# A one-core trunk layer: 512-column gate products over four token tiles, the last layer norm tiles on VectorE, state-space products later in the queue

## The chip, the cores and the metric

The kernel runs as one program on one core of a Trainium2 chip. The metric is device time in microseconds. A profiled execution gives one trace with a span from its first to its last instruction; the timed runs are taken without a profile. Engines: TensorE (PE in rows, PEld for its weight loads), VectorE (DVE), ScalarE (ACT), GpSimd (POOL), SyncE (SP, which issues the DMAs).

## The reference, cut to what matters

One layer on x (1024 tokens x 1024), all float32. `z = x @ w_in` gives the streams of three branches: u and v (512 wide) with a gate g for the gated MLP, x_b with its gate for the state-space branch, q with its gate for attention over 256 memory tokens.

```python
def spatial_gating(u, v, w_s, b_s, ln_g, ln_b, causal):
    vh = layer_norm(v.reshape(Bsz, L, GM_HEADS, GM_HEAD_DIM), ln_g, ln_b)
    ...
    mixed = jnp.einsum('hts,bcshd->bcthd', w, vc) + b_s.T[None, None, :, :, None]
    return u * mixed.reshape(Bsz, L, GM_WIDTH)
...
        z = x @ w_in[layer]
        u_a, v_a, g_a, x_b, g_b, q_x, g_x = jnp.split(z, SPLITS, axis=-1)
        y_a = spatial_gating(jax.nn.gelu(u_a), jax.nn.gelu(v_a), ...)
        y_b = s5_branch(x_b, ...)
        y_x = memory_cross_attention(q_x, mem, xa_w_k[layer], xa_w_v[layer])
        y = jnp.concatenate([y_a * jax.nn.silu(g_a), y_b * jax.nn.silu(g_b),
                             y_x * jax.nn.silu(g_x)], axis=-1)
        x = layer_norm(DN_ALPHA * x + y @ w_out[layer], ln_g[layer], ln_b[layer])
```

The layer norm inside the spatial gate is per head (4 heads of 128 channels) and the mixing is per chunk of 128 tokens and head; in the state-space branch there are 16 groups of 64 complex states.

## The kernel before

Every large product is made of three matmuls with operands in the fp32r type (`mm3`, lines 144 to 146): a value is split into a high part (a cast on ScalarE, line 65) and a low part (a subtraction on VectorE, line 62), and high x high, high x low and low x high are summed in a PSUM bank. Weights come in **pieces** of 128 x 512: a load on SP, then the cast and the subtraction. There are four raw buffers and six pairs of high and low buffers, used in turn.

The input projection runs as **units** one after the other (`run_units`). A unit made by `fm` computes 128 channels for all 1024 tokens: weights stationary, 512 tokens moving, two z banks (there are four, used in turn; four more u banks serve everything else). A unit made by `tm` computes 256 gate channels v: a 128-token tile of x stationary, 256 weight columns moving; two token tiles share one bank, and the bank is finished (16 x 3 matmuls) before the next is begun. Its four pieces, two k tiles each, are needed for every token tile. The order of units is xb0, xb1, gb0, gb1, v0, u0, u1, g0, g1, v1, u2, u3, g2, g3, where gb is the state-space branch's gate, u and g those of the gated MLP.

Between the matmuls of units other work is put in by generators: at each `tick` a virtual clock `now` moves on, and generators whose time has come emit their next step. They are the attention (during xb and gb), the state-space batches (`ssm_batch`, four of them; pp and kp, then up, then yp are their matmuls; H is the state that yp reads, and comes from up through some ten VectorE steps), the normalisation and mixing of v (`mix_all`, matmuls mx), and the state-space gate (`glu_all`, matmuls gl; its operands yth and ytl come from yT, a copy of the transposes yt). `yield 4.0` says how far `now` must move until a step. The emission fixes TensorE's order; in this stage the order on the other engines and on SP is made by the scheduler of the framework. During the output projection the order is the written one on VectorE, ScalarE and GpSimd too.

`v_evac` takes a finished v bank: Gelu on ScalarE into `nv`, then statistics on VectorE, four instructions of each of two kinds. `mix_all` normalises in sixteen 128 x 128 steps on VectorE, after a power on GpSimd, and mixes.

The output projection goes over the columns 0 to 511 in eight banks at once, k by k (o0), then over columns 512 to 1023 tile by tile (o10 to o16), and for the last token tile in two quarters of 256 (o170, o171). `o_part` adds the residual and takes statistics, `finish_a(t)` aggregates, has GpSimd take the power, and multiplies; `finish_b(t)` scales, adds the bias and stores. For tiles 0 to 5 it scales on ScalarE and adds on GpSimd; tile 6 is done on VectorE in two halves; of tile 7, columns 864 to 1023 go by way of ScalarE and GpSimd and the rest is done on VectorE.

Of the kernel before, what the change touches and what calls it, by code (L numbers as in the profile page):

```python
# [36 lines left out]
def trunk_kernel(ctx, tc, xT, x, w_gq, w_kv, memT, w_fm, w_v, w_o,  # L37
# [127 lines left out]
    class Unit:  # L165
        def __init__(self, name, src, count, run):
            self.name, self.src, self.count, self.run = name, src, count, run
            self.pcs = []
# [6 lines left out]
    def run_units(units, after):  # L175
        for i, u in enumerate(units):
            u.fetch()
            u.run(u, units[i + 1] if i + 1 < len(units) else after)
# [470 lines left out]
    for hp in range(2):  # L649
        for lt in range(8):  # L650
# [5 lines left out]
    v_units = [tm(w_v[:, vb], f"v{vb}",  # L656
                  lambda t, kt: (xh[:, kt, tok[t]], xl[:, kt, tok[t]]),
                  lambda tt, ps, vb=vb: v_evac(vb, tt, ps), lambda vb=vb: v_done(vb))
               for vb in range(2)]
# [19 lines left out]
    def ssm_batch(bi):  # L679
# [80 lines left out]
        yield 4.0  # L760
# [70 lines left out]
    def v_evac(vb, tt, ps):  # L831
        if tt == 0:
            nv[vb] = gm.tile([P, 8, 256], F32, tag="nv", name=f"nv{vb}")
            stt[vb] = (gm.tile([P, 16, 6], F32, tag="stt", name=f"stt{vb}"),
                       gm.tile([P, 16, 2], F32, tag="mv", name=f"mv{vb}"),
                       gm.tile([P, 16], F32, tag="rsv", name=f"rsv{vb}"))
        t = nv[vb]
        st, mv, _ = stt[vb]
        S.activation(t[:, 2 * tt:2 * tt + 2].rearrange("p c f -> p (c f)"), ps,
                     AF.Gelu_apprx_tanh)  # L840
        for i in range(4 * tt, 4 * tt + 4):
            V.bn_stats(st[:, i], t[:, i // 2, tok[i % 2]])
        for i in range(4 * tt, 4 * tt + 4):
            V.bn_aggr(mv[:, i], st[:, i])

    def v_done(vb):
        spawn(mix_all(vb))

    def mix_all(vb):
        t = nv[vb]  # L850
        _, mv, rs = stt[vb]
# [3 lines left out]
        for h in range(2):  # L855
            for c in range(8):
                i = c * 2 + h
                sl = t[:, c, tok[h]]
                V.tensor_scalar(sl, sl, mv[:, i, 0:1], rs[:, i:i + 1], op0=ALU.subtract,
                                op1=ALU.mult)  # L860
            yield 2.0
        yield 4.0
        for h in range(2):
            hd = vb * 2 + h
            while hd not in have_u:
                yield 1.0
            for cq in range(2):
                ps = ubank(f"mx{hd}{cq}")
                for c in range(4):
                    T.matmul(ps[:, tok[c]], lhsT=t[:, cq * 4 + c, tok[h]], rhs=wT[:, hd],  # L870
                             start=(c == 0), stop=(c == 3), skip_group_check=True)
                now[0] += 0.85
                mt = gm.tile([P, 4, P], F32, tag="mt", bufs=2, name=f"mt{hd}{cq}")
                V.scalar_tensor_tensor(mt, ps.rearrange("p (c t) -> p c t", c=4),
                                       gmg[:, hd:hd + 1],
                                       tbias[:, hd].unsqueeze(1).to_broadcast([P, 4, P]),
                                       op0=ALU.mult, op1=ALU.add)
                mul(V, ya[:, hd, half[cq]], ya[:, hd, half[cq]], mt.rearrange("p c t -> p (c t)"))
                yield 2.0
# [19 lines left out]
    run_units([v_units[0], us[0], us[1], gs_[0], gs_[1], v_units[1], us[2], us[3]], gs_[2])  # L899
# [36 lines left out]
    def finish_a(t, n):  # L936
        mv, rs = stat[:, 192 + 4 * t:194 + 4 * t], stat[:, 194 + 4 * t:195 + 4 * t]
        V.bn_aggr(mv, ost[:, t, 0:n].rearrange("p a b -> p (a b)"))
        V.tensor_scalar(rs, mv[:, 1:2], LN_EPS, None, op0=ALU.add)  # L939
        G.tensor_tensor(rs, rs, nhalf[:, 0:1], op=ALU.pow)  # L940
        w = 864 if t == 7 else 1024
        V.scalar_tensor_tensor(res[:, t, :w], res[:, t, :w], mv[:, 0:1], lng[:, :w],
                               op0=ALU.subtract, op1=ALU.mult)

    def finish_b(t):
        rs = stat[:, 194 + 4 * t:195 + 4 * t]
        ot = res[:, t]
        if t < 6:
            S.activation(ot, ot, AF.Copy, scale=rs)  # L949
            add(G, ot, ot, lnb2)  # L950
            nc.sync.dma_start(out=out[tok[t]], in_=ot)
            return
        cuts = ((0, 512), (512, 1024)) if t == 6 else ((864, 1024), (0, 432), (432, 864))
        for a, b in cuts:
            if b - a > 160:
                V.scalar_tensor_tensor(ot[:, a:b], ot[:, a:b], rs, lnb2[:, a:b],
                                       op0=ALU.mult, op1=ALU.add)
            else:
                nm = stat[:, 195 + 4 * t:196 + 4 * t]
                V.scalar_tensor_tensor(nm, stat[:, 192 + 4 * t:193 + 4 * t], -1.0, rs,  # L960
                                       op0=ALU.mult, op1=ALU.mult)
# [71 lines left out]
def _layout(np, x, mem, w_in, gm_w_s, gm_b_s, gm_ln_g, gm_ln_b, ssm_lam_re, ssm_lam_im,  # L1033
# [14 lines left out]
    def both(a):  # L1048
# [13 lines left out]
        w_v=np.stack([cols(w[:, 512:768]), cols(w[:, 768:1024])], axis=1),  # L1062
# [39 lines left out]
```

## Time and profile before

| | us |
|---|---|
| median of 3 runs | 391.1 |
| lowest and highest run | 391.07, 392.14 |
| profiled execution | 391.75 |
| its span | 389.9 |

| engine | busy us | share of the span |
|---|---|---|
| TensorE, matmuls | 379.0 | 97% |
| TensorE, weight loads | 329.8 | 85% |
| VectorE | 267.5 | 69% |
| ScalarE | 155.0 | 40% |
| GpSimd | 101.1 | 26% |

Times of rows count from the start of the span. Matmuls are pipelined, so a row's own duration is longer than its share of the queue: what one costs is the distance between the starts of neighbours. Weight loads run beside matmuls. An engine runs its instructions in order; the wait of one holds up those behind it.

### The profile page before, as it was taken

The page shows a single profiled execution, that of the slowest core. Times are in us where ns is not written, and L with a number is a line of the kernel's source. Part 1 is how long each engine was busy: PE and PEld are TensorE (multiplying, and loading weights), DVE is VectorE, ACT ScalarE, POOL GpSimd, SP SyncE. Part 2 cuts the span into 40 slices and gives each one's busy share as a digit, 9 for nine tenths or more (in the row PEclk, how much of TensorE's full clock was granted, in tenths as well). Part 3 has the DMA queues.
Part 4 walks back from the last instruction along what each step waited for, and adds up shares of the span by engine and source line. Part 5 has one row for each costly group of instructions (what it writes and reads, how often), then busy time and mean ns, then how long its engine had stood idle before and what let it go on. Part 6 is the DMA issues. An engine that isn't in the chain of part 4 may idle for free.

```text
span 389.9 us, 5809 instructions
## 1 busy us (share of the span) xinstructions
PE 379.0 (97%) x2129; PEld 329.8 (85%) x2129; DVE 267.5 (69%) x580; ACT 155.0 (40%) x301; POOL 101.1 (26%) x80
## 2 busy tenths in 40 slices
PE   8999999999999999999999999999999999999990
PEld 6888898888888999888889999888888888888890
DVE  4599897888884689699769258855357410974475
ACT  4573596667673723131153224216346410012210
POOL 1315000000000865803936402300000000026763
PEclk9999999999999999999999999999999999999996
DMA  7883336312930100312111003200138710002124
GB/s 235 274 280 128 114 109 191 109 71 78 114 62 28 29 13 3 109 31 70 51 43 55 2 15 109 108 2 2 53 109 319 283 46 0 0 2 83 79 110 161
DMA packets 22189, 35.89 MB, mean 92 GB/s; under 512 B 5376, under 2 KB 8848, under 8 KB 22032
## 3 DMA queue, kind: packets, MB, share of 16 engines
q1 hardware_dynamic: 22160, 35.51, 29.9%
q8 instruction: 17, 0.28, 0.3%
q14 instruction: 12, 0.10, 0.1%
HBM read 29.67 MB, written 5.24 MB: 90 GB/s over the span
## 4 chain that ended last, share of the span: by engine, by line
PE 94%; POOL 2%; issue 1%; DMA 1%; DVE 1%; SPq 0%; POOLq 0%; ACT 0%
PE o L146 7%; PE o L145 7%; PE o L144 7%; PE zv L145 4%; PE zv L144 4%; PE zv L146 4%; PE zu L152 4%; PE zu L151 4%; PE zg L152 4%; PE zg L151 4%; PE zu L154 4%; PE zg L154 4%; PE av L615 2%; PE zgb L152 2%; PE zgb L154 2%; PE zxb L152 2%
## 5 line engine op out<-in xcount | busy, mean ns | idle before, releaser
L940 POOL TENSOR_TENSOR stat<-stat,nhalf 128x1 f32<-128x1 f32 x8 | 11.9, 1490 | 105.2 <-DVE stat L939 105.2
L145 PE MATMUL o<-l_wo,yh 128*128 128x512 f32 (+1 forms) x100 | 38.4, 384 | 0.0
L144 PE MATMUL o<-h_wo,yh 128*128 128x512 f32 (+1 forms) x100 | 38.4, 384 | 0.0
L146 PE MATMUL o<-h_wo,yl 128*128 128x512 f32 (+1 forms) x100 | 38.3, 383 | 0.0
L144 PE MATMUL zv<-h_v,xh 128*128 128x256 f32 x128 | 36.7, 286 | 0.0
L145 PE MATMUL zv<-l_v,xh 128*128 128x256 f32 x128 | 36.3, 283 | 0.0
L146 PE MATMUL zv<-h_v,xl 128*128 128x256 f32 x128 | 36.3, 283 | 0.0
L151 PE MATMUL zu<-xh,h_u 128*128 128x512 f32 x64 | 25.8, 403 | 0.0
L151 PE MATMUL zg<-xh,h_g 128*128 128x512 f32 x64 | 25.5, 399 | 0.0
L152 PE MATMUL zu<-xl,h_u 128*128 128x512 f32 x64 | 25.1, 391 | 0.0
L152 PE MATMUL zg<-xl,h_g 128*128 128x512 f32 x64 | 25.0, 391 | 0.0
L145 PEld LDWEIGHTS zv<-l_v,xh 128*128 128x128 f32 x128 | 24.6, 192 | 0.1
L144 PEld LDWEIGHTS zv<-h_v,xh 128*128 128x128 f32 x128 | 24.6, 192 | 0.1
L146 PEld LDWEIGHTS zv<-h_v,xl 128*128 128x128 f32 x128 | 24.5, 192 | 0.0
L968 DVE SCALAR_TENSOR_TENSOR res<-res,o 128x512 f32<-128x512 f32 (+1 forms) x16 | 10.3, 646 | 19.0 <-PE o L146 19.0
L949 ACT ACTIVATE res<-res,stat 128x1024 f32<-128x1024 f32 x6 | 6.9, 1152 | 41.0 <-POOL stat L940 41.0
L146 PEld LDWEIGHTS o<-h_wo,yl 128*128 128x128 f32 x100 | 18.8, 188 | 3.9
L145 PEld LDWEIGHTS o<-l_wo,yh 128*128 128x128 f32 x100 | 18.8, 188 | 3.9
L144 PEld LDWEIGHTS o<-h_wo,yh 128*128 128x128 f32 x100 | 18.8, 188 | 3.9
L154 PE MATMUL zu<-xh,l_u 128*128 128x512 f32 x64 | 19.8, 390 | 0.0
L154 PE MATMUL zg<-xh,l_g 128*128 128x512 f32 x64 | 19.8, 390 | 0.0
L676 POOL MEMSET M<- 128x512 f32 x2 | 1.0, 526 | 66.7 <-PE zgb L152 66.7
(301 smaller groups left out, 1073.2 us busy)
## 6 DMA issues: line engine op xcount, KB each, us to landing
r_wo<-in_w_o_dram SPq DMA_DIRECT2D x16, 256.0 KB, 3.0
res<-in_x_dram SPq DMA_DIRECT2D x8, 512.0 KB, 7.1
r_x<-in_xT_dram SPq DMA_DIRECT2D x15, 256.0 KB, 4.6
out_dram<-res SPq DMA_DIRECT2D x6, 512.0 KB, 2.6
r_v<-in_w_v_dram SPq DMA_DIRECT2D x8, 256.0 KB, 3.1
r_u<-in_w_fm_dram SPq DMA_DIRECT2D x8, 256.0 KB, 2.8
r_g<-in_w_fm_dram SPq DMA_DIRECT2D x8, 256.0 KB, 2.7
r_wgq<-in_w_gq_dram SPq DMA_DIRECT2D x7, 256.0 KB, 5.3
```

What stands on the lines that cost most here:

```text
L144: T.matmul(ps, lhsT=sh, rhs=mh, start=start, stop=False, **kw)
L145: T.matmul(ps, lhsT=sh, rhs=ml, start=False, stop=False, **kw)
L146: T.matmul(ps, lhsT=sl, rhs=mh, start=False, stop=stop, **kw)
L151: T.matmul(ps[h], lhsT=wh, rhs=xh[:, kt, half[h]], start=first, stop=False, **kw[h])
L152: T.matmul(ps[h], lhsT=wh, rhs=xl[:, kt, half[h]], start=False, stop=False, **kw[h])
L154: T.matmul(ps[h], lhsT=wl, rhs=xh[:, kt, half[h]], start=False, stop=last, **kw[h])
L615: T.matmul(ps[:, h * 256:h * 256 + 256], lhsT=vs[:, m, 2 * hp + h], rhs=pp[:, h * 2 + m], start=h + m + n == 0, stop=h + m + n == 3, skip_ ...
L676: G.memset(t, 0.0)
L940: G.tensor_tensor(rs, rs, nhalf[:, 0:1], op=ALU.pow)
L949: S.activation(ot, ot, AF.Copy, scale=rs)
L968: V.scalar_tensor_tensor(res[:, t, c0:c0 + w], res[:, t, c0:c0 + w], ALPHA, ps[:, :w], op0=ALU.mult, op1=ALU.add)
```

## The change

The gate units are cut the other way: a unit `vu(h)` computes all 512 channels of v for four token tiles (512 tokens), with 512 weight columns moving and four banks open; six k tiles run over all four tiles, the last two are run tile by tile, so that the banks finish one after the other. A piece is now one k tile with 512 columns; there are eight in a unit, fetched a few steps ahead of their use, and the weights are read once by each unit. The units are ordered v0, u0, u1, u2, u3, v1, g0, g1, g2, g3. Normalising and mixing follow the new cut. The wait ahead of yp is 6.0 in place of 4.0. In the tail tiles 0 to 4 are done as before, tile 5 on VectorE in one step, tile 6 on VectorE in two halves, tile 7 on VectorE in three pieces of 480, 352 and 192 columns.

```diff
     class Unit:
-        def __init__(self, name, src, count, run):
+        def __init__(self, name, src, count, run, ahead=8):
...
-            u.fetch()
+            u.fetch(u.ahead)
             u.run(u, units[i + 1] if i + 1 < len(units) else after)
...
-    def tm(src, name, stat, evac, done=None):
+    def vu(h, evac, done):
+
+
         def run(u, nxt):
-            for tt in range(4):
-                ps = zbank(f"z{name}{tt}")
-                for t2 in range(2):
-                    for kt in range(KT):
-                        wh, wl = u.pcs[kt // 2]
-                        cs = slice((kt % 2) * 256, (kt % 2) * 256 + 256)
-                        sh, sl = stat(2 * tt + t2, kt)
-                        mm3(ps[:, t2 * 256:t2 * 256 + 256], sh, sl, wh[:, cs], wl[:, cs],
-                            kt == 0 and t2 == 0, kt == KT - 1 and t2 == 1, chk=True)
...
-                            tick(1.3)
-                if tt in (1, 2) and nxt is not None:
-                    nxt.fetch(tt)
-        return Unit(name, lambda i: src[:, i], 4, run)
+            ps = [zbank(f"zv{h}{t}") for t in range(4)]
+
+            def mm(t, kt):
+                ts = slice((4 * h + t) * P, (4 * h + t) * P + P)
+                mm3(ps[t], xh[:, kt, ts], xl[:, kt, ts], *u.pcs[kt], kt == 0, kt == KT - 1)
+
+            for kt in range(KT - 2):
+                u.fetch(kt + 4)
+                for t in range(4):
+                    mm(t, kt)
+                    if t % 2:
+                        tick(1.36)
+            for t in range(4):
+                for kt in (KT - 2, KT - 1):
+                    mm(t, kt)
+                evac(t, ps[t])
+                if t == 3:
+                    done()
+                tick(1.36)
+                if t in (1, 2) and nxt is not None:
+                    nxt.fetch(t)
+        return Unit(f"v{h}", lambda i: w_v[:, i], KT, run, 4)
...
         add(V, H[:, :, 1:P], H[:, :, 1:P], jg[:, :, 0:P - 1])
-        yield 4.0
+        yield 6.0
         yps = ubank(f"yp{bi}")
...
+    def v_evac(th, t, ps):
...
+        S.activation(v[:, t], ps, AF.Gelu_apprx_tanh)
+        for i in range(4 * t, 4 * t + 4):
+            V.bn_stats(st[:, i], v[:, t, tok[i % 4]])
+        for i in range(4 * t, 4 * t + 4):
             V.bn_aggr(mv[:, i], st[:, i])
...
-    run_units([v_units[0], us[0], us[1], gs_[0], gs_[1], v_units[1], us[2], us[3]], gs_[2])
+    run_units([v_units[0], *us, v_units[1], gs_[0], gs_[1]], gs_[2])
...
-        w = 864 if t == 7 else 1024
-        V.scalar_tensor_tensor(res[:, t, :w], res[:, t, :w], mv[:, 0:1], lng[:, :w],
-                               op0=ALU.subtract, op1=ALU.mult)
+        V.scalar_tensor_tensor(res[:, t], res[:, t], mv[:, 0:1], lng, op0=ALU.subtract,
+                               op1=ALU.mult)
...
-        if t < 6:
+        if t < 5:
             S.activation(ot, ot, AF.Copy, scale=rs)
             add(G, ot, ot, lnb2)
             nc.sync.dma_start(out=out[tok[t]], in_=ot)
             return
-        cuts = ((0, 512), (512, 1024)) if t == 6 else ((864, 1024), (0, 432), (432, 864))
-        for a, b in cuts:
...
-                S.activation(ot[:, a:b], ot[:, a:b], AF.Identity, bias=nm, scale=rs)
-                mul(G, ot[:, a:b], ot[:, a:b], lng[:, a:b])
-                add(G, ot[:, a:b], ot[:, a:b], lnb2[:, a:b])
+        cuts = {5: (0, 1024), 6: (0, 512, 1024), 7: (0, 480, 832, 1024)}[t]
+        for a, b in zip(cuts, cuts[1:]):
+            V.scalar_tensor_tensor(ot[:, a:b], ot[:, a:b], rs, lnb2[:, a:b], op0=ALU.mult,
+                                   op1=ALU.add)
             nc.sync.dma_start(out=out[tok[t], a:b], in_=ot[:, a:b])
...
-        w_v=np.stack([cols(w[:, 512:768]), cols(w[:, 768:1024])], axis=1),
+        w_v=kpart(w[:, 512:1024]),
```

On TensorE, where the first v unit follows gb1 (zgb10 and zgb11 are gb1's two banks, zv00 and so on those of v0, h and l the high and low part of a piece), before:

```order
L154 MATMUL zgb10_1465<-xh_88,l_gb1_1_1336 128x512
L154 MATMUL zgb11_1466<-xh_88,l_gb1_1_1336 128x512
L144 MATMUL zv00_1619<-h_v0_0_1518,xh_88 128x256
L145 MATMUL zv00_1619<-l_v0_0_1519,xh_88 128x256
L146 MATMUL zv00_1619<-h_v0_0_1518,xl_89 128x256
L144 MATMUL zv00_1619<-h_v0_0_1518,xh_88 128x256
```

and in the changed kernel:

```order
L154 MATMUL zgb10_1465<-xh_88,l_gb1_1_1336 128x512
L154 MATMUL zgb11_1466<-xh_88,l_gb1_1_1336 128x512
L144 MATMUL zv00_1619<-h_v0_0_1518,xh_88 128x512
L145 MATMUL zv00_1619<-l_v0_0_1519,xh_88 128x512
L146 MATMUL zv00_1619<-h_v0_0_1518,xl_89 128x512
L144 MATMUL zv01_1620<-h_v0_0_1518,xh_88 128x512
L145 MATMUL zv01_1620<-l_v0_0_1519,xh_88 128x512
L146 MATMUL zv01_1620<-h_v0_0_1518,xl_89 128x512
L144 MATMUL zv02_1621<-h_v0_0_1518,xh_88 128x512
```

The third bank, which takes the place of zgb10's, is written by the seventh matmul of the unit, where before it was the ninety-seventh.

On ScalarE at the same place (yb is where gb1 is copied to, h_u0_1 and h_v0_5 are casts of pieces), before:

```order
L820 ACT_TABLE_LOAD
L820 ACTIVATE yb_92<-yb_92 128x512 x2
L65 CAST h_u0_1_1876<-r_u0_1_1874 128x512
L222 COPY yb_92<-zgb10_1465 128x512
L222 COPY yb_92<-zgb11_1466 128x512
L820 ACTIVATE yb_92<-yb_92 128x512 x2
L839 ACT_TABLE_LOAD
L839 ACTIVATE nv0_1680<-zv00_1619 128x512
```

and in the changed kernel:

```order
L826 ACT_TABLE_LOAD
L826 ACTIVATE yb_92<-yb_92 128x512 x2
L65 CAST h_v0_5_1697<-r_v0_5_1695 128x512
L229 COPY yb_92<-zgb10_1465 128x512
L229 COPY yb_92<-zgb11_1466 128x512
L826 ACTIVATE yb_92<-yb_92 128x512 x2
L65 CAST h_v0_6_1716<-r_v0_6_1714 128x512
L65 CAST h_v0_7_1753<-r_v0_7_1751 128x512
```

The copies of gb1's banks stand where they stood; the cast ahead of them is another piece's.

On VectorE at the end of the program, from the multiplication of tile 6 on, before:

```order
L942 SCALAR_TENSOR_TENSOR res<-res,stat,lnp 128x1024
L968 SCALAR_TENSOR_TENSOR res<-res,o_3777 128x256
L970 BN_STATS stat<-res 128x6
L956 SCALAR_TENSOR_TENSOR res<-res,stat,lnp 128x512 x2
L968 SCALAR_TENSOR_TENSOR res<-res,o_3808 128x256
L970 BN_STATS stat<-res 128x6
L938 BN_AGGR stat<-stat 128x2
L939 TENSOR_SCALAR stat<-stat 128x1
L942 SCALAR_TENSOR_TENSOR res<-res,stat,lnp 128x864
L960 SCALAR_TENSOR_TENSOR stat<-stat 128x1
L956 SCALAR_TENSOR_TENSOR res<-res,stat,lnp 128x432 x2
```

and in the changed kernel, from the step after that multiplication:

```order
L957 SCALAR_TENSOR_TENSOR res<-res,stat,lnp 128x1024
L962 SCALAR_TENSOR_TENSOR res<-res,o_3632 128x256
L964 BN_STATS stat<-res 128x6
L957 SCALAR_TENSOR_TENSOR res<-res,stat,lnp 128x512 x2
L962 SCALAR_TENSOR_TENSOR res<-res,o_3663 128x256
L964 BN_STATS stat<-res 128x6
L941 BN_AGGR stat<-stat 128x2
L942 TENSOR_SCALAR stat<-stat 128x1
L944 SCALAR_TENSOR_TENSOR res<-res,stat,lnp 128x1024
L957 SCALAR_TENSOR_TENSOR res<-res,stat,lnp 128x480
L957 SCALAR_TENSOR_TENSOR res<-res,stat,lnp 128x352
L957 SCALAR_TENSOR_TENSOR res<-res,stat,lnp 128x192
```

A step of 1024 columns for tile 5 has come in ahead of tile 7's first quarter, and tile 7 ends with three pieces on this engine.

## Rows read from the trace of the kernel before

**Rows 1.** The page: busy us by engine; granted TensorE clock in 40 slices, tenths.
```profile
PE 379.0 (97%) x2129; PEld 329.8 (85%) x2129; DVE 267.5 (69%) x580; ACT 155.0 (40%) x301; POOL 101.1 (26%) x80
...
PEclk9999999999999999999999999999999999999996
```

**Rows 2.** Waits of TensorE: who, for whom, us in total, times, longest.
```profile
PE warm L236 <- DVE warm L233: 1.1, 1, 1.1
PE gx L145 <- DVE xl L62: 0.6, 1, 0.6
```

**Rows 3.** Stretches: length, busy us PE, PEld, DVE, ACT, POOL, clock, DMA share, GB/s.
```profile
128.40:153.70 25.30, 25.30 (x214) 25.28 (x213) 20.66 (x50) 9.92 (x17) 18.04 (x16) 1.00 0.07 17
290.00:340.00 50.00, 50.00 (x219) 40.92 (x218) 21.61 (x35) 12.09 (x22) 0.00 (x0) 1.00 0.37 134
```

**Rows 4.** Timeline of TensorE in v0 (start, us, engine, line, operation): first matmul, first transpose.
```profile
128.42 0.28 PE L144 MATMUL zv<-h_v,xh 128*128 128x256 f32 x1
...
135.61 0.27 PE L710 MATMUL pp<-ident,L 128*128 128x128 f32 x1
```

**Rows 5.** Timeline of TensorE: first matmuls of o16, o170 and o171.
```profile
369.63 0.39 PE L144 MATMUL o<-wb_h,yh 128*128 128x512 f32 x1
...
375.13 0.28 PE L144 MATMUL o<-wb_h,yh 128*128 128x256 f32 x1
...
377.97 0.28 PE L144 MATMUL o<-wb_h,yh 128*128 128x256 f32 x1
```

**Rows 6.** Timeline of ScalarE as v0 begins.
```profile
128.99 0.60 ACT L65 CAST h_u<-r_u 128x512 fp32r<-128x512 f32 x1
129.62 0.59 ACT L222 COPY yb<-zgb 128x512 f32<-128x512 f32 x1
```

**Rows 7.** Timeline of VectorE and TensorE: the end of H, its first reader.
```profile
152.05 1.49 DVE L59 TENSOR_TENSOR H<-H,jg 128x508 f32<-128x508 f32 x1
...
156.61 0.28 PE L765 MATMUL yp<-Q,H 128*128 128x128 f32 x1
```

**Rows 8.** Timeline of VectorE: both normalisations, the copies of yt, a subtraction.
```profile
163.13 6.92 DVE L859 TENSOR_SCALAR nv<-nv,mv,rsv 128x128 f32<-128x128 f32 x16 [3.02 <-POOL rsv L853]
...
243.16 0.69 DVE L62 TENSOR_TENSOR ytl<-yT,yth 128x512 fp32r<-128x512 f32 x1 [1.76 <-PE yp L765]
244.43 4.20 DVE L859 TENSOR_SCALAR nv<-nv,mv,rsv 128x128 f32<-128x128 f32 x16 [0.58 <-POOL rsv L853]
248.53 2.10 DVE L781 COPY yT<-yt 128x512 f32<-128x512 f32 x2
```

**Rows 9.** Timelines of the tail: TensorE's last matmul, VectorE, GpSimd, SP.
```profile
380.70 0.28 PE L146 MATMUL o<-h_wo,yl 128*128 128x256 f32 x1
...
377.10 1.28 DVE L942 SCALAR_TENSOR_TENSOR res<-res,stat,lnp 128x1024 f32<-128x1024 f32 x1
378.29 0.42 DVE L968 SCALAR_TENSOR_TENSOR res<-res,o 128x256 f32<-128x256 f32 x1
...
379.08 2.62 DVE L956 SCALAR_TENSOR_TENSOR res<-res,stat,lnp 128x512 f32<-128x512 f32 x1
381.62 0.74 DVE L956 SCALAR_TENSOR_TENSOR res<-res,stat,lnp 128x512 f32<-128x512 f32 x1
382.28 0.41 DVE L968 SCALAR_TENSOR_TENSOR res<-res,o 128x256 f32<-128x256 f32 x1
...
385.18 1.24 DVE L956 SCALAR_TENSOR_TENSOR res<-res,stat,lnp 128x432 f32<-128x432 f32 x2
...
377.26 1.52 POOL L940 TENSOR_TENSOR stat<-stat,nhalf 128x1 f32<-128x1 f32 x1 [1.60 <-DVE stat L939]
378.75 2.40 POOL L59 TENSOR_TENSOR res<-res,lnp 128x1024 f32<-128x1024 f32 x1
383.72 1.36 POOL L940 TENSOR_TENSOR stat<-stat,nhalf 128x1 f32<-128x1 f32 x1 [2.57 <-DVE stat L939]
...
386.88 0.52 POOL L59 TENSOR_TENSOR res<-res,lnp 128x160 f32<-128x160 f32 x1
...
387.43 0.33 SPq L965 DMA_DIRECT2D out_dram<-res  x1
```

More of the change, by code (lines that the diff above doesn't have):

```diff
@@ L165, in trunk_kernel @@
     class Unit:
-        def __init__(self, name, src, count, run):
+        def __init__(self, name, src, count, run, ahead=8):
             self.name, self.src, self.count, self.run = name, src, count, run
+            self.ahead = ahead
             self.pcs = []
@@ L265, in trunk_kernel @@
     class KV:
+        ahead = 2
         def __init__(self):
@@ L655, in trunk_kernel @@
     gb1 = fm(1, "gb1", raw_to(yb, 1))
[L656 to L659, printed above, removed]
+    v_units = [vu(h, lambda t, ps, h=h: v_evac(h, t, ps), lambda h=h: v_done(h)) for h in range(2)]
     run_units([*xb, gb0, gb1], v_units[0])
@@ L829, in trunk_kernel, with v_done, mix_all @@
     stt = {}
[L831 to L843, printed above, removed]
-            V.bn_aggr(mv[:, i], st[:, i])
[L846 to L851, printed above, removed]
+    def v_evac(th, t, ps):
+        if t == 0:
+            nv[th] = gm.tile([P, 4, 512], F32, tag="nv", name=f"nv{th}")
+            stt[th] = (gm.tile([P, 16, 6], F32, tag="stt", name=f"stt{th}"),
+                       gm.tile([P, 16, 2], F32, tag="mv", name=f"mv{th}"),
+                       gm.tile([P, 16], F32, tag="rsv", name=f"rsv{th}"))
+        v = nv[th]
+        st, mv, _ = stt[th]
+        S.activation(v[:, t], ps, AF.Gelu_apprx_tanh)
+        for i in range(4 * t, 4 * t + 4):
+            V.bn_stats(st[:, i], v[:, t, tok[i % 4]])
+        for i in range(4 * t, 4 * t + 4):
+            V.bn_aggr(mv[:, i], st[:, i])
+    def v_done(th):
+        spawn(mix_all(th))
+    def mix_all(th):
+        v = nv[th]
+        _, mv, rs = stt[th]
         V.tensor_scalar(rs, mv[:, :, 1], LN_EPS, None, op0=ALU.add)
@@ L854, in mix_all @@
         yield 5.0
[L855 to L858, printed above, removed]
+        for hd in range(4):
+            for c in range(4):
+                i = c * 4 + hd
+                sl = v[:, c, tok[hd]]
                 V.tensor_scalar(sl, sl, mv[:, i, 0:1], rs[:, i:i + 1], op0=ALU.subtract,
                                 op1=ALU.mult)
-            yield 2.0
+            yield 1.0
         yield 4.0
-        for h in range(2):
-            hd = vb * 2 + h
+        for hd in range(4):
             while hd not in have_u:
                 yield 1.0
[L867 to L879, printed above, removed]
+            ps = ubank(f"mx{hd}{th}")
+            for c in range(4):
+                T.matmul(ps[:, tok[c]], lhsT=v[:, c, tok[hd]], rhs=wT[:, hd],
+                         start=(c == 0), stop=(c == 3), skip_group_check=True)
+            now[0] += 0.85
+            mt = gm.tile([P, 4, P], F32, tag="mt", bufs=2, name=f"mt{hd}{th}")
+            V.scalar_tensor_tensor(mt, ps.rearrange("p (c t) -> p c t", c=4),
+                                   gmg[:, hd:hd + 1],
+                                   tbias[:, hd].unsqueeze(1).to_broadcast([P, 4, P]),
+                                   op0=ALU.mult, op1=ALU.add)
+            mul(V, ya[:, hd, half[th]], ya[:, hd, half[th]], mt.rearrange("p c t -> p (c t)"))
+            yield 2.0
     have_u = set()
```

12 lines of the change are left out of this document (removed).

## The prediction

> **What bounds the kernel now.** I read the page's busy shares first, then who TensorE waited for, then the stretches, then single rows. TensorE is busy 97% of the span at a granted clock of full speed in nearly every slice [rows 1], and the few times it waits lie in the first 8 us, the largest 1.1 us [rows 2]. So the time is a plain sum: 7 us of start, then one unbroken queue of matmuls, then about 9 us from the last matmul (380.98, [rows 9]) to the end of the span (389.9). VectorE is busy 20.66 of 25.30 us in the first v unit [rows 3] without stopping TensorE. Only three things can therefore move the time: the length of the matmul queue, a wait that the new order puts into it, and the tail.
>
> **The change part by part.**
>
> *512 columns instead of 256.* Before, a v unit is 192 matmuls of 256 columns, after it is 96 of 512. Between the first one (128.42) and the first transpose (135.61) stand 60 of the old form, 0.1198 us each [rows 4]. The new form, 512 columns with another stationary tile at each step, is what the output projection runs: 24 between 369.63 and 375.13, 0.2292 us each [rows 5]. Two units: 384 x 0.1198 = 46.0 us become 192 x 0.2292 = 44.0 us, a gain of **2.0 us**, all of it on the path. Bounds: the output projection's own 256-column form takes (377.97 - 375.13)/24 = 0.1183 us [rows 5], by which the gain would be 1.4 us, and I allow the same 0.6 the other way, 2.6. I take 2.0, since it sets the old form as this unit runs it against the new form as another unit runs it.
> A rule of the Trainium skill says less: "TensorE: Matmul & The Clock Gate", section "Back-to-back issue gap", gives a warm matmul its columns over 2.4 GHz plus a fixed 2.5 ns. By it the two units would save 192 x 2.5 ns, an estimated 0.5 us. [Rows 4] and [rows 5] show 2 x 0.1198 - 0.2292 = 0.0104 us per pair, four times that, so I weigh it only as a rival.
>
> *Four token tiles at once.* A v unit now needs four z banks within its first twelve matmuls. The third (zv02) and fourth are those of gb1, whose evacuation is queued on ScalarE behind an activation table, two Silu and a cast (the order of ScalarE shows the same four in front before and after). That cast starts at 128.99 and the first copy runs from 129.62 to 130.21 [rows 6]. zv02 would start six matmuls after 128.42, at 128.42 + 6 x 0.229 = 129.80. So TensorE waits **0.4 us**, a wait that the trace of before doesn't have; its old unit touched one bank at a time. The fourth bank comes 0.7 us later on both sides and adds nothing. At v1 the same banks belong to u3; there a 0.9 us group of mixing matmuls stands between u3 and v1, and cast and copies (0.60 + 2 x 0.59 us, [rows 6]) are done before zv12 is reached 2.3 us after u3. Leaving a v unit is easy: its first bank is finished 4 us before the next unit wants it.
>
> *Twice the weight pieces.* w_v is now read by each unit: 16 pieces for 8, so 8 more loads on SP, 8 more casts of about 0.6 us on ScalarE and 8 more subtractions on VectorE. A piece lasts 12 x 0.229 = 2.75 us on TensorE and is fetched three pieces ahead, so a load, a cast and a subtraction have 8 us. I cost it at nothing; the cover is the idle VectorE of [rows 3] (18% of the first v unit), and three of that unit's four groups of statistics move behind H, out of the way.
>
> *State-space products later.* In the queue, yp0 stands after two steps of u0 as before. From up0 to yp0 there are 60 matmuls of 512 (13.7 us) where there were 84 of 256 and 12 of 512 (12.8 us), so H gets 0.9 us more; the other three batches get 0.5 to 0.9. Before, H was done at 153.54 and its first reader started at 156.61 [rows 7], 3.1 us to spare. On VectorE one group of statistics leaves this chain and two subtractions enter it. The second needs a weight buffer that TensorE frees 24 matmuls (5.5 us) after up0; with its cast (0.60), itself (0.7) and H's last addition at the slow price (1.49) that is 8.3 us after up0, 5 us before yp0. I expect no wait.
>
> *Order of units.* u0 to u3 now follow v0 and the second mixing falls among g1 and the gate of the state-space branch. The tight place is gl00's fifth matmul, which reads ytl01. It comes 40 matmuls of 0.229 us, 9.2 us, after the transposes yt11. In this time VectorE does the yT copies (2.10 us, 0.4 of them under the transposes), 15 of 16 normalisations (16 took 4.20 us alone and 6.92 us beside GpSimd) and one subtraction of 0.7 [rows 8]: 6.3 to 8.9 us. Spare 0.3 to 2.9 us; cost 0, at worst about 1 us.
>
> *The tail.* GpSimd's addition of tile 5 (378.75, 2.40 us) made VectorE's first half of tile 6 take 2.62 us where the second took 0.74 [rows 9]. In the new order that addition is gone and VectorE does tile 5 itself. From 378.29: tile 5 takes 1.19 (the distance of the 1024-column rows 377.10 and 378.29), the first quarter of tile 7 with its statistics 0.79 (378.29 to 379.08), tile 6's halves 2 x 0.66: the second quarter of tile 7 starts at 378.29 + 1.19 + 0.79 + 1.32 = 381.59, not 382.28 (0.69 gained; TensorE's end, 380.98, allows 0.6 more). From there statistics and power take 2.80 us as before (382.28 to 385.08); then three pieces of 480, 352 and 192 columns on VectorE at about 0.63 + 0.50 + 0.41 = 1.54 us (from 432 columns in 0.66 and 0.58 apart) and the last store is issued about 0.1 us later, 4.49 us after that quarter began. Before it was 387.43 - 382.28 = 5.15 us, by way of ScalarE and two GpSimd steps (0.52 us the last). That is 0.66 more. The rest, store to end, is 2.5 us in both. Gain **1.35 us**. Bounds: 0.7 if VectorE's quarter starts no earlier, 1.9 if it starts as TensorE ends.
>
> **The sum**, against the profiled execution (391.75 us, of which 389.9 span): -2.0 + 0.4 - 1.35 = -2.95, so 388.8. The median of the runs shown, 391.1, lies 0.65 below that execution; the forecast is **388.2 us**.
>
> **The rivals.**
> *The tail gives only half.* VectorE now carries 1.19 us more before tile 7's last quarter; if its steps cost what they cost beside GpSimd's power (1.52 us long there), the quarter starts no earlier, and three stores issued close together land later. Against it: the 1024-column row beside that power is no slower than its width says. 391.1 - 2.0 + 0.4 = 389.5.
> *A wait at the gate.* The normalisation runs at its slow price and ytl01 comes late, or a late piece stops a v unit: about 1.5 us. For it: [rows 8], 0.3 us to spare at the upper end. 389.7.
> *The matmul saves only a fixed issue cost.* The 0.0104 us per pair belong to the stage and not to the count. The 256-column rows of the output projection point half way there. With a quarter of the gain, 391.1 - 0.5 + 0.4 - 1.35 = 389.7. This is where the page's rule above would lead.
> *Slower: the H chain.* The casts and subtractions of pieces now stand inside the chain from up to H. VectorE steps beside GpSimd take up to 1.49 us where 0.7 is usual [rows 7]; each such step delays H by 0.8. It decides from five such steps in one batch (3.1 us to spare and 0.9 more); with seven in each of four batches TensorE waits 4 x 1.6 = 6.4 us: 388.2 + 6.4 = 394.6. Against it: statistics leave the chain and the chain has more matmuls in front of its reader.
> *The clock falls.* Each unit moves through four banks, three matmuls at a time. In 290 to 340 us the output projection moves through eight banks in just this way, at a granted clock of 1.00 [rows 3], the 2.4 GHz level. At 1.2 GHz the 192 matmuls would take twice as long, 432 us. The Trainium skill tells of such a case (same page, "A second HAM failure mode: psum-queue depth-cycling": cycling through PSUM banks let the clock swing between its levels); by that rule this change would be the wrong way round, and the trace speaks against it.
> *It does not do what it says.* The products are not later by any count of u0's steps, as said; the other two parts are in the order in full.
>
> **How the numbers follow.** Forecast 0.62 (386.8 to 389.2: below, the larger matmul and tail gains, -2.6 + 0.4 - 1.9, short of a little; above, the smaller matmul gain and half a microsecond more of waiting); half a tail 0.13; wait at the gate 0.10; fixed cost only 0.08; slower by the H chain 0.05; clock 0.02. A measurement of this kernel tells about 0.3% (1.2 us) from no change, so faster means below 389.9. The forecast's case is all there, the three at 389.5 to 389.7 lie close to the line and I give two thirds of their 0.31 to faster: faster 0.82, same 0.11, slower 0.07. The range runs from 386.8 to 390.2, which takes in those three with some spread and leaves the last two out.
>
> **What would show it.** In the changed trace: the zv matmuls start 0.229 us apart and there are 192; the list of TensorE's waits has one new entry, zv after ScalarE's copy of gb1 at about 130 us, some 0.4 us; the last matmul starts 1.6 us earlier, near 379.1; VectorE's last quarter of tile 7 begins 0.6 us after TensorE's end where it was 1.3; no VectorE row of the tail is over 1.3 us; the last store is issued near 384.5. It would be wrong if TensorE waited for H, ytl or a v piece for more than 1 us in sum, or if the zv pitch stayed at 0.240 us per 512 columns.

## The result and the profile after

The changed kernel takes **389.26 us** (median of 8 runs, 388.28 to 389.6) beside 391.35 us for the kernel before in the same comparison (8 runs); the ratio is 0.9931, 95% interval 0.9909 to 0.9953. Run once more beside other kernels (below) it took 388.77 us beside 391.23, ratio 0.9943 (0.9929 to 0.9956). The forecast was 388.2 us, range 386.8 to 390.2. One execution of half_cols below took 983.94 us, TensorE alone being slower at a granted clock shown as 1.00, and is left out of that kernel's median and ratio and of the table.

The profiled execution has a span of 386.5 us (388.28 us in all) where the kernel before had 389.9. First the page of the changed kernel, busy us by engine and the granted clock, to be read against [rows 1], then all its waits of TensorE, against [rows 2]:

```profile
PE 377.0 (98%) x1937; PEld 319.9 (83%) x1937; DVE 273.7 (71%) x589; ACT 155.6 (40%) x305; POOL 97.6 (25%) x77
...
PEclk9999999999999999999999999999999999999997
```

```profile
PE warm L243 <- DVE warm L240: 1.1, 1, 1.1
PE zv L144 <- ACT yb L229: 0.3, 1, 0.3
```

TensorE has 192 instructions fewer, the clock is granted in full as before, and behind the start there is one single new wait, the one at the third z bank. Around it, from the timeline of TensorE (start, us, engine, line, operation, with the idle time ahead in brackets), and the last matmul of the kernel, which answers the first row of [rows 9]:

```profile
128.71 0.39 PE L146 MATMUL zv<-h_v,xl 128*128 128x512 f32 x1
129.42 0.50 PE L144 MATMUL zv<-h_v,xh 128*128 128x512 f32 x1 [0.32 <-ACT yb L229]
129.75 0.40 PE L145 MATMUL zv<-l_v,xh 128*128 128x512 f32 x1
129.99 0.39 PE L146 MATMUL zv<-h_v,xl 128*128 128x512 f32 x1
...
378.18 0.28 PE L146 MATMUL o<-h_wo,yl 128*128 128x256 f32 x1
```

One matmul normally starts 0.23 us after the one before. Here the step is 0.71 us, and the one behind it 0.33: the stop adds 0.48 us to the first step and about 0.1 to the next, though the bracket says 0.32.

The tail answers [rows 9]: VectorE, GpSimd, and SP (its last two stores, the second issued at 383.72):

```profile
375.76 1.28 DVE L957 SCALAR_TENSOR_TENSOR res<-res,stat,lnp 128x1024 f32<-128x1024 f32 x1
...
377.75 1.40 DVE L957 SCALAR_TENSOR_TENSOR res<-res,stat,lnp 128x512 f32<-128x512 f32 x2
379.06 0.41 DVE L962 SCALAR_TENSOR_TENSOR res<-res,o 128x256 f32<-128x256 f32 x1
...
380.34 1.28 DVE L944 SCALAR_TENSOR_TENSOR res<-res,stat,lnp 128x1024 f32<-128x1024 f32 x1
382.06 1.54 DVE L957 SCALAR_TENSOR_TENSOR res<-res,stat,lnp 128x480 f32<-128x480 f32 x3 [0.44 <-POOL stat L943]
...
380.50 1.52 POOL L943 TENSOR_TENSOR stat<-stat,nhalf 128x1 f32<-128x1 f32 x1 [4.25 <-DVE stat L942]
...
383.30 0.84 SPq L959 DMA_DIRECT2D out_dram<-res  x2
```

The 2.62 us row of VectorE is gone: both halves of tile 6 take 1.40 us together, and the last quarter of tile 7 begins 0.61 us after TensorE's end (378.45) instead of 1.30.

Beside the last matmul's own 0.28 us, every profiled span falls into three pieces: up to the first zv matmul, from there to the start of the last matmul (the **queue** below), and from the end of that one to the end of the span (the **tail**). Here they are for eleven executions (us; the names are those of the experiments below; spans are given to 0.1, so the tail is good to 0.05).

| kernel | first zv matmul | to the last matmul | its end to end of span | span |
|---|---|---|---|---|
| before | 128.42 | 252.28 | 8.92 | 389.9 |
| changed | 127.58 | 250.60 | 8.05 | 386.5 |
| changed, once more | 127.83 | 250.60 | 8.09 | 386.8 |
| v_only | 127.79 | 250.59 | 8.94 | 387.6 |
| tail_only | 127.64 | 252.29 | 8.09 | 388.3 |
| half_cols_2 | 127.69 | 252.81 | 8.13 | 388.9 |
| silu_late | 128.32 | 249.98 | 8.12 | 386.7 |
| yield4 | 128.85 | 253.12 | 8.15 | 390.4 |
| split_tail | 127.72 | 250.60 | 7.70 | 386.3 |
| best | 127.68 | 249.99 | 7.76 | 385.7 |
| best_two | 127.94 | 249.99 | 7.69 | 385.9 |

Between executions whose edits leave them alone, the second and third pieces repeat to 0.02 and 0.1 us. The first moves by 1.3 us with no edit in it. Two places make this: in the first 8 us TensorE waits a varying time for casts and splits ([rows 2] shows one such wait of 0.6 us, the rows above none), so that q's first matmul starts between 7.81 and 8.82 us; and about 38 us a matmul of gx can wait for a split on VectorE, which in yield4 below makes a step of 1.05 us (38.05 to 39.10) where best has 0.23. In yield4's list of waits it is this one:

```profile
PE gx L152 <- DVE xl L62: 0.7, 1, 0.7
```

Between the kernel before and the changed one all 0.84 us come from the first place. So of the 3.4 us between the two profiled spans, 0.84 are chance, 1.68 are the queue of matmuls and 0.87 the tail.

### The profile page after: what moved, and what is told of

It is laid out like the page before. It is cut to its first block, busy times and chain, and to the rows that moved or that the text cites. A ratio compares the mean times of both kernels' runs of the same rounds, so it can differ in the third digit from the quotient of the medians.

```text
span 386.5 us, 5465 instructions
## 1 busy us (share of the span) xinstructions
PE 377.0 (98%) x1937; PEld 319.9 (83%) x1937; DVE 273.7 (71%) x589; ACT 155.6 (40%) x305; POOL 97.6 (25%) x77
## 4 chain that ended last, share of the span: by engine, by line
PE 94%; issue 1%; ACT 1%; DVE 1%; DMA 1%; POOLq 0%; POOL 0%; SPq 0%; DVEq 0%
PE o L145 7%; PE o L146 7%; PE o L144 7%; PE zu L151 4%; PE zu L152 4%; PE zg L151 4%; PE zu L154 4%; PE zg L152 4%; PE zg L154 4%; PE zv L144 4%; PE zv L146 4%; PE zv L145 4%; PE av L624 2%; PE zxb L152 2%; PE zxb L154 2%; PE zxb L151 2%
## 5 line engine op out<-in xcount | busy, mean ns | idle before, releaser
L144 PE MATMUL zv<-h_v,xh 128*128 128x512 f32 x64 | 25.6, 400 | 0.3 <-ACT yb L229 0.3
L146 PE MATMUL zv<-h_v,xl 128*128 128x512 f32 x64 | 24.9, 390 | 0.0
L145 PE MATMUL zv<-l_v,xh 128*128 128x512 f32 x64 | 24.9, 389 | 0.0
L62 DVE TENSOR_TENSOR l_v<-r_v,h_v 128x512 fp32r<-128x512 f32 x16 | 15.6, 978 | 7.2 <-ACT h_v L65 7.1
L65 ACT CAST h_v<-r_v 128x512 fp32r<-128x512 f32 x16 | 9.9, 620 | 26.4 <-PE zu L152 18.4
L951 ACT ACTIVATE res<-res,stat 128x1024 f32<-128x1024 f32 x5 | 5.8, 1152 | 36.6 <-POOL stat L943 36.6
L596 ACT ACTIVATE pr<-s,nm 128x256 f32<-128x256 f32 x32 | 14.9, 472 | 7.9 <-DVE nm L592 6.5
L62 DVE TENSOR_TENSOR l_wo<-r_wo,h_wo 128x512 fp32r<-128x512 f32 x12 | 8.0, 689 | 14.0 <-ACT h_wo L65 13.9
```

Source lines behind the costliest of these rows:

```text
L62: eng.tensor_tensor(o, a, b, op=ALU.subtract)
L65: S.copy(hi, src)
L144: T.matmul(ps, lhsT=sh, rhs=mh, start=start, stop=False, **kw)
L145: T.matmul(ps, lhsT=sh, rhs=ml, start=False, stop=False, **kw)
L146: T.matmul(ps, lhsT=sl, rhs=mh, start=False, stop=stop, **kw)
L596: S.activation(pr[:, h], ps3[:, h], AF.Exp, bias=nm[:, h:h + 1], scale=1.0, accum_out=rs[:, h:h + 1])
```

## The experiments

**The two halves apart.** v_only is the changed kernel with the old tail:

```diff
-        if t < 5:
+        if t < 6:
...
-        cuts = {5: (0, 1024), 6: (0, 512, 1024), 7: (0, 480, 832, 1024)}[t]
+        cuts = ((0, 512), (512, 1024)) if t == 6 else ((864, 1024), (0, 432), (432, 864))
```

> The changed kernel with the layer norm tail of the kernel before (tile 5 by ScalarE and GpSimd, tile 7 partly by ScalarE and GpSimd). Theory (the two halves add up): from the first zv matmul to the last matmul 250.6 us as in the changed kernel (252.3 before), with the 0.5 us stop at the third zv bank; from the last matmul's end to the end of the span 8.9 us as before, with the 2.6 us row of VectorE back; time 1.7 us under the kernel before (ratio 0.996). Rival (the tail carries it all, the shorter queue only moves the waiting into the tail): 252.3 us or a tail over 9.5 us, and a ratio of 1.000.

Measured: 390.04 us beside 391.21, ratio 0.9960 (0.9944 to 0.9976). Queue 250.59, tail 8.94, as the theory had it. VectorE's rows of the tail show the old obstacle again, tile 6's halves in 3.28 us where the changed kernel has 1.40:

```profile
375.97 0.41 DVE L971 SCALAR_TENSOR_TENSOR res<-res,o 128x256 f32<-128x256 f32 x1
376.42 0.43 DVE L973 BATCH_NORM_STATS2 stat<-res 128x6 f32<-128x256 f32 x1
376.76 3.28 DVE L959 SCALAR_TENSOR_TENSOR res<-res,stat,lnp 128x512 f32<-128x512 f32 x2
```

tail_only is the kernel before with the new tail, the same diff the other way round.

> The kernel before with only the new tail (tiles 5 to 7 by VectorE alone). Theory: the queue of matmuls stays as before (252.3 us from the first zv matmul to the last); VectorE's last quarter of tile 7 starts 0.6 us after the last matmul instead of 1.3, its power ends 0.4 us behind a 1024-column step of 1.28 us, and from the last matmul's end to the end of the span it is 8.05 us instead of 8.92: 0.9 us faster (ratio 0.998). Rival (half a tail, or none): the quarter starts no earlier and the tail is 8.7 us or more, ratio 1.000.

Measured: 390.4 us beside 391.21, ratio 0.9975 (0.9962 to 0.9987); queue 252.29, tail 8.09. The last matmul started at 379.93; the rows of VectorE behind it:

```profile
380.82 0.41 DVE L959 SCALAR_TENSOR_TENSOR res<-res,o 128x256 f32<-128x256 f32 x1
...
382.10 1.28 DVE L941 SCALAR_TENSOR_TENSOR res<-res,stat,lnp 128x1024 f32<-128x1024 f32 x1
383.83 1.54 DVE L954 SCALAR_TENSOR_TENSOR res<-res,stat,lnp 128x480 f32<-128x480 f32 x3 [0.46 <-POOL stat L940]
```

The halves add up: 0.9960 x 0.9975 = 0.9935, between the two measurements of the whole. Both rivals fall.

**The changed kernel once more**, for the part that is chance.

> The changed kernel once more, unaltered, beside the others of this row. Theory (the difference of the two profiled executions, 3.4 us, holds 0.84 us that lies ahead of the first zv matmul and comes and goes with the landing of the first loads): first zv matmul to last matmul 250.6 us, last matmul to end of span 8.05 us, both to 0.1; the start of the zv matmuls anywhere between 127.6 and 128.4 us; 2.6 us under the kernel before (ratio 0.9935). Rival (the start belongs to the change): zv starts at 127.6 again.

Measured: 388.77 us, ratio 0.9943 (0.9929 to 0.9956), first zv matmul at 127.83, queue 250.60, tail 8.09. The start lies between the two guesses. That it is chance rests on all eleven starts of the table: tail_only, with the matmuls of the kernel before, starts zv at 127.64, and yield4, with those of the changed kernel up to there, at 128.85.

**The columns alone.** half_cols keeps the new loop, its loads, banks and order, and writes each 512-column matmul as two of 256.

```diff
-                mm3(ps[t], xh[:, kt, ts], xl[:, kt, ts], *u.pcs[kt], kt == 0, kt == KT - 1)
+                wh, wl = u.pcs[kt]
+                for c in range(2):
+                    cs = slice(c * 256, c * 256 + 256)
+                    mm3(ps[t][:, cs], xh[:, kt, ts], xl[:, kt, ts], wh[:, cs], wl[:, cs],
+                        kt == 0 and c == 0, kt == KT - 1 and c == 1, chk=True)
```

> The changed kernel with each 512-column zv matmul written as two of 256 columns into the halves of the same bank; loads, order, banks and tail stay. Theory (the gain comes from the number of matmuls): the zv pitch goes from 0.227 us per 512 columns to 2 x 0.1195 = 0.239, so 192 x 0.011 = 2.1 us come back, and the time is 2.1 us above the changed kernel, 0.6 us under the kernel before. Rival (the gain per pair belongs to the old unit's order of visits, or is a fixed 2.5 ns per instruction): 0 to 0.5 us above the changed kernel.

Measured: 390.93 us (eleven executions) beside 391.21, ratio 0.9993 (0.9980 to 1.0007). The profile that goes with the theory is that of a second run of the same kernel:

> The changed kernel with each 512-column zv matmul written as two of 256 columns, again, for its profile. Theory: 384 zv matmuls at 0.119 to 0.120 us, 2.1 to 2.3 us more from the first zv matmul to the last matmul than in the changed kernel (252.8 against 250.6), tail as in the changed kernel; 2.1 us above it. Rival (the pair costs a fixed 2.5 ns each): 0.5 us above it.

Measured: 390.97 us, ratio 0.9994 (0.9983 to 1.0005); beside the changed kernel in the same comparison (388.77) 2.2 us more. The queue is 252.81 us, 2.21 more, with the stop at the third bank a little shorter. The first zv matmuls, and the last matmul of all:

```profile
127.69 0.28 PE L144 MATMUL zv<-h_v,xh 128*128 128x256 f32 x1
127.80 0.28 PE L145 MATMUL zv<-l_v,xh 128*128 128x256 f32 x1
127.92 0.28 PE L146 MATMUL zv<-h_v,xl 128*128 128x256 f32 x1
128.04 0.28 PE L144 MATMUL zv<-h_v,xh 128*128 128x256 f32 x1
...
380.50 0.28 PE L146 MATMUL o<-h_wo,yl 128*128 128x256 f32 x1
```

So the gain belongs to the number of matmuls and to nothing else of the new unit: 2.21 us over 192 pairs, 0.0115 us a pair. Every matmul brings its own weight load; which of the two costs the 0.0115 us isn't shown. With the columns halved again, the queue is 0.53 us longer than before, about what the stop costs there, and this uses up most of the tail's gain: the ratio is 0.999.

**The stop at the third bank.** silu_late puts gb1's copies out of PSUM ahead of the activation table and gb0's and gb1's Silu on ScalarE.

```diff
-        return lambda h, ps: S.copy(dst[:, f, half[h]], ps)
+        def ev(h, ps):
+            last_gb[0] = S.copy(dst[:, f, half[h]], ps)
+        return ev
...
-                with tc.issue_after(last_att[0].ins):
+                with tc.issue_after(last_att[0].ins), tc.issue_after(last_gb[0].ins):
```

> The changed kernel with gb1's two copies put ahead of the activation table and the Silu of gb0 on ScalarE, so that the third and fourth zv banks come free earlier. Theory: the copies run from about 127.6 to 128.8 us, the third bank is free at 128.2, before its first matmul at 128.9, the only stop of TensorE (0.48 us) goes and nothing else comes in its place; 0.5 us less than the changed kernel. Rival: the table load (1.28 us) and the four Silu now delay the casts of the v pieces or the state-space inputs, TensorE waits later instead, and the time is that of the changed kernel or above.

Measured: 388.19 us beside 391.21, ratio 0.9915 (0.9896 to 0.9934). ScalarE's timeline, and the matmul that stopped before:

```profile
128.06 0.62 ACT L65 CAST h_v<-r_v 128x512 fp32r<-128x512 f32 x1 [1.54 <-PE zgb L152]
128.71 1.07 ACT L230 COPY yb<-zgb 128x512 f32<-128x512 f32 x2
129.80 1.28 ACT L830 ACT_TABLE_LOAD   x1
131.10 2.20 ACT L830 ACTIVATE yb<-yb 128x512 f32<-128x512 f32 x4
...
129.68 0.39 PE L144 MATMUL zv<-h_v,xh 128*128 128x512 f32 x1
```

A cast still goes first, so the copies come later than I had written, but the first one is done before TensorE reaches the bank (six matmuls after 128.32). The list of waits has nothing behind the start, and the queue is 249.98 us: 250.60 - 249.98 = 0.62 us is what the stop cost, not the 0.3 of the list nor the 0.48 of the step.

**The later place of the state-space products.** yield4 takes the third edit back.

```diff
-        yield 6.0
+        yield 4.0
         yps = ubank(f"yp{bi}")
```

> The changed kernel with the old distance (4 instead of 6) from H to the state-space output products: each of the four groups yp stands 12 matmuls (2.75 us) earlier in TensorE's queue. Theory (the later place is needed): in the changed kernel H's last addition ended 1.97, 1.24, 4.20 and 3.84 us before its first reader; 2.75 us earlier the first two groups wait, for 0.8 and about 0.7 to 1.5 us, the other two don't; 0.8 to 2.3 us above the changed kernel. Rival (H has time enough, as the prediction had it from the 3.1 us of the first group before): no wait, same time as the changed kernel.

Measured: 391.45 us, ratio 1.0003 (0.9990 to 1.0016), 2.7 us above the changed kernel of the same comparison. TensorE's list of waits has a new first entry; below it the two places in TensorE's timeline, and in VectorE's the row that the first of them waits for, with the subtraction ahead of it:

```profile
PE yp L771 <- DVE H L59: 2.1, 2, 1.4
```

```profile
154.64 0.46 PE L771 MATMUL yp<-Q,H 128*128 128x128 f32 x2 [0.73 <-DVE H L59]
...
183.95 0.46 PE L771 MATMUL yp<-Q,H 128*128 128x128 f32 x2 [1.38 <-DVE H L59]
...
151.44 1.57 DVE L62 TENSOR_TENSOR l_u<-r_u,h_u 128x512 fp32r<-128x512 f32 x1
152.93 1.56 DVE L59 TENSOR_TENSOR H<-H,jg 128x508 f32<-128x508 f32 x1
```

The theory holds in place, and the two waits have the sizes that it gave (0.73 and 1.38 us). What they cost is more than its 0.8 to 2.3 us: 2.52 in the queue, 2.7 in the median. Without the third edit the first two lose the whole gain.

**The power in the tail.** split_tail cuts tile 7's centring step in three.

```diff
-        V.scalar_tensor_tensor(res[:, t], res[:, t], mv[:, 0:1], lng, op0=ALU.subtract,
-                               op1=ALU.mult)
+        if t < 7:
+            centre(t, 0, 1024)
+        else:
+            centre(7, 0, 480)
+            centre(7, 480, 832)
...
             nc.sync.dma_start(out=out[tok[t], a:b], in_=ot[:, a:b])
+            if t == 7 and a == 0:
+                centre(7, 832, 1024)
```

> The changed kernel with tile 7's centring step of 1024 columns on VectorE cut into 480, 352 and 192, the last one moved behind the first finished piece, so that GpSimd's power can come between them. Theory (GpSimd's power gets to its data only between two VectorE instructions, and ends 0.4 us behind the one it stood beside): the power ends 0.4 us behind the 480-column piece, about 0.6 us earlier, VectorE waits for nothing, the last store is issued 0.2 to 0.4 us earlier; time 0.3 us less than the changed kernel. Rival (the power needs its 1.4 to 1.5 us whatever VectorE does, or waits for the end of the whole row of pieces): it ends 0.4 us behind the 352-column piece or later, and the last store is not earlier.

Measured: 388.06 us beside 388.77 for the changed kernel in the same comparison, ratio to before 0.9918 (0.9905 to 0.9931). VectorE and GpSimd:

```profile
380.49 1.21 DVE L951 SCALAR_TENSOR_TENSOR res<-res,stat,lnp 128x480 f32<-128x480 f32 x2
381.63 0.72 DVE L965 SCALAR_TENSOR_TENSOR res<-res,stat,lnp 128x480 f32<-128x480 f32 x1
382.27 0.41 DVE L951 SCALAR_TENSOR_TENSOR res<-res,stat,lnp 128x192 f32<-128x192 f32 x1
...
380.65 0.95 POOL L943 TENSOR_TENSOR stat<-stat,nhalf 128x1 f32<-128x1 f32 x1 [4.25 <-DVE stat L942]
```

The same power of 128 numbers took 1.52 us beside a step of 1.28 us and takes 0.95 beside one of 0.71; both times it ends 0.40 us behind that step (380.50 + 1.52 against 380.34 + 1.28; 380.65 + 0.95 against 380.49 + 0.71). VectorE loses its wait of 0.44 us, the last store is issued at 383.63, 5.03 us after TensorE's end instead of 5.27, and the tail is 7.70, 0.35 to 0.39 us less than in the two executions of the changed kernel. That is the theory's 0.3; the rest of the 0.71 us between the medians is no more than the scatter of the start. The rival falls.
The Trainium skill has a rule for this: "SBUF — State Buffer", section "SBUF: two separate sides", says that a GpSimd instruction and a VectorE instruction with two SBUF inputs share a port pair as an exclusive lock, and that the one which comes second is blocked for the whole of the other. The trace agrees for the power behind VectorE's step, and in [rows 9] for VectorE's 2.62 us row behind GpSimd's addition of 2.40. For the VectorE step behind the power it shows no such block: the first two pieces take 1.21 us together, and so do the same widths at the end of the changed kernel (382.06 to 383.27), where GpSimd does nothing.

**Both repairs together.** best is silu_late with the tail of split_tail; best_two has two pieces instead of three at the end.

```diff
-        cuts = {5: (0, 1024), 6: (0, 512, 1024), 7: (0, 480, 832, 1024)}[t]
+        cuts = {5: (0, 1024), 6: (0, 512, 1024), 7: (0, 480, 1024)}[t]
```

> The changed kernel with both repairs: gb1's copies ahead of the Silu of gb0 on ScalarE, and tile 7's centring step in three pieces. Theory (the two are independent): no wait of TensorE behind 8 us, 250.0 us from the first zv matmul to the last; 7.7 to 7.8 us from the last matmul's end to the end of the span; 0.6 + 0.3 = 0.9 us less than the changed kernel, 3.4 us under the kernel before (ratio 0.9905). Rival (the gains overlap, or the earlier copies were start jitter): 0.993.

> The same with two pieces (480 and 544 columns) instead of three in tile 7's last steps and stores. Theory (a piece costs 0.14 us beside its columns, and a third store close behind the second lands 0.3 us later behind its issue than it would alone): VectorE ends 0.3 us earlier after the last matmul, the last store is issued 4.75 us after it instead of 5.03 and lands 2.0 us later; 0.1 to 0.2 us less than with three pieces. Rival (the larger last store lands later by its size): the same as with three pieces or slower.

Measured beside 391.23 us: best 387.62, ratio 0.9897 (0.9867 to 0.9927); best_two 387.53, ratio 0.9891 (0.9858 to 0.9923). TensorE's waits in best are down to the one at the start of the kernel:

```profile
PE warm L247 <- DVE warm L244: 1.1, 1, 1.1
```

The two repairs add up (queue 249.99, tail 7.76) and make a version that is below both kernels: 3.6 us under the kernel before in the median, and under the changed kernel, which did not run beside it, by 0.61 us of queue and about 0.3 of tail. With two pieces the last store is issued 4.65 us after TensorE's end, 0.38 earlier, but lands 2.09 us later instead of 1.85; the tails, 7.69 and 7.76, can't be told apart, and why a last store lands 1.7 to 2.1 us behind its issue stays open.

## Why the prediction was right, and where its terms were off

Direction and mechanism held: a shorter queue with one stop in it, and a shorter tail, and 389.26 us within 386.8 to 390.2. The time alone would not have told: it lies just above the forecast's own case (386.8 to 389.2) and nearer to the rivals at 389.5 to 389.7 than to 388.2. The traces tell. The sum was -2.95; they give -1.68 - 0.87 = **-2.55**. That the queue came out at -1.68 for -1.6 is partly luck: a gain of 0.3 more and a stop of 0.2 more nearly cancel.

*512 columns.* Forecast -2.0. Without the stop, the queue became 2.3 us shorter (252.28 to 249.98, silu_late), and half_cols_2 says the same from the other side. The mis-sized factor is the pitch of the old unit: I took its first 60 matmuls, 0.1198 us. Over all stretches of zv in both units the old form ran at 0.1209 (46.4 us for 384), the new one at 0.2302 without the stop (44.2 for 192). The rival of the fixed issue cost (0.5 us) is out.
By the Trainium skill's formula in "TensorE: Matmul & The Clock Gate", section "Back-to-back issue gap", which the section gives for matmuls without the weight loads of a real kernel, a pair would save 2.5 ns; half_cols_2 measured 11.5.

*Four token tiles at once.* The wait came where it was forecast, for the instruction that was named. I gave it 0.4 us; the step was 0.48 us longer, the next one about 0.1, and the cost in the queue 0.62.

*Twice the weight pieces.* No wait for a piece, so the term of zero held, but the idle VectorE that was to cover it (18% in [rows 3]) was used up, as the row of the first v unit shows:

```profile
127.58:152.23 24.65, 24.33 (x118) 20.12 (x116) 24.14 (x31) 12.26 (x21) 18.21 (x15) 1.00 0.25 71
```

VectorE is busy 24.14 of 24.65 us there.

*State-space products.* "No wait" was right, "5 us before yp0" was not. The rows that answer [rows 7]:

```profile
151.65 1.56 DVE L59 TENSOR_TENSOR H<-H,jg 128x508 f32<-128x508 f32 x1
...
155.18 0.39 PE L771 MATMUL yp<-Q,H 128*128 128x128 f32 x2
```

2.0 us are left, 1.1 less than before: from up0 (140.42) the products come 14.54 us later instead of 13.71 (the third of them is the first to read H, 0.22 us on), but H is ready 12.79 us later instead of 10.86. The step that failed is the count of subtractions: four stood between up0 and H, not two, and the three that ran beside GpSimd cost 1.56 to 1.77 us, not 0.7:

```profile
140.86 3.25 DVE L62 TENSOR_TENSOR l_u<-r_u,h_u 128x512 fp32r<-128x512 f32 x2
147.36 0.67 DVE L62 TENSOR_TENSOR l_u<-r_u,h_u 128x512 fp32r<-128x512 f32 x1
150.16 1.56 DVE L62 TENSOR_TENSOR l_u<-r_u,h_u 128x512 fp32r<-128x512 f32 x1
```

I also read the slack at the first batch alone; at the second one H ended 0.8 us before its reader even in the kernel before (first two rows), and 1.2 us in the changed one (last two):

```profile
183.72 1.56 DVE L59 TENSOR_TENSOR H<-H,jg 128x508 f32<-128x508 f32 x1
186.11 0.28 PE L765 MATMUL yp<-Q,H 128*128 128x128 f32 x1
...
180.22 1.45 DVE L59 TENSOR_TENSOR H<-H,jg 128x508 f32<-128x508 f32 x1
182.91 0.28 PE L771 MATMUL yp<-Q,H 128*128 128x128 f32 x1
```

So "no wait" came true although its working failed: 2.0 and 1.2 us of slack were left where it had 5. The rival "H chain" had the mechanism right, and yield4 shows that it was near: 2.75 us less distance costs 2.5 us of the queue.

*The gate.* The tight place held with 0.8 us (forecast 0.3 to 2.9): the first of VectorE's two ytl rows ends at 249.54, gl00's fifth matmul starts at 250.31.

```profile
248.85 0.69 DVE L62 TENSOR_TENSOR ytl<-yT,yth 128x512 fp32r<-128x512 f32 x1
...
250.31 0.39 PE L145 MATMUL gl<-ytl,gwh 128*128 128x512 f32 x1
```

*The tail.* Forecast 1.35, measured 0.87. The first half was exact: the quarter starts 0.61 us after TensorE's end (0.69 gained). Of the second half, 0.66, only 0.18 came. The failed step is "statistics and power take 2.80 us as before": tile 7's centring step grew from 864 to 1024 columns, 1.11 to 1.28 us, the power ends 0.40 us behind it, and all that follows moved by 0.17. The other 0.31 is "store to end, 2.5 us in both": it was 2.78, the last store landing 1.99 us behind its issue instead of 1.66. That is what the rival "half a tail" spoke of, for a quarter of the term; its time, 389.5, leaves out the whole tail, and with half of it would be 388.8. Two sums of the working are also off by a little: 2.80 + 1.54 + 0.1 is 4.44 and not 4.49, and -2.6 + 0.4 - 1.9 leads to 387.0 and not 386.8.

*Clock, and whether it does what it says.* The granted clock is 1.00 in the first v unit, in the row above as in [rows 3], so that rival is out; and that the products do stand later, and must, is what yield4 shows.

The median then lay 1.06 us above the forecast: 0.40 from these terms, 0.25 because the kernel before ran at 391.35 this time and not 391.1, and the remaining 0.4 is no more than the scatter ahead of the first zv matmul. The second comparison gave 2.46 us between the medians, near the 2.55 of the traces.

## What to carry to other kernels

When one engine is never idle, make fewer and wider instructions on it, and then look for the instruction whose output buffer the wider tiling needs earlier: that one stop cost a quarter of the gain, and a reordering on another engine gave it back. Pushing a reader back in the queue makes room for a producer chain that has grown; read the slack of every repetition, not of the first alone, and price VectorE's elementwise steps by what they cost beside GpSimd where the two run together. In a tail, do not let a tiny instruction on GpSimd queue behind a wide one on VectorE: cut the wide one.

## What the runs showed of the hardware that was not expected

- A power of 128 single numbers on GpSimd ends 0.40 us behind the VectorE step it stands beside (it takes 0.95, 1.36 and 1.52 us beside steps of 0.71, 1.11 and 1.28), and slips in between two VectorE instructions without a visible loss to them (480 and 352 columns together 1.21 us with it and without).
- The one stop of TensorE in the queue cost more than the trace's waiting time: 0.32 us in the bracket, 0.48 between matmuls, 0.62 in the length of the queue.
- From the first v unit to the last matmul the queue repeats to 0.02 us between executions of the same matmuls; nearly all scatter of the profiled time lies ahead of it, in the first 8 us and about 38 us, and it is as large (1.3 us) as the effects measured here.
